# Layer 0's dense mixer of a two-layer trunk: both token streams in one pass over w1 and w3

## The chip, the cores and the metric

One NeuronCore of a Trainium2 chip runs the whole program. The metric is the device time of one execution in microseconds. A time is the median of several executions; the profile is of one more execution, and its span is counted from the first to the last instruction in it. Engines are named as in the profile: PE (products; PEld its weight loads), DVE and ACT (elementwise work), POOL, and SP, whose queue issues most DMAs.

## The reference, cut to what matters

Two streams of 256 tokens with 1024 features, the context and the latents, pass through a two-layer trunk. In a layer each stream is normed and modulated, goes through a token mixer (attention, a recurrence "RWKV", and a long convolution "Hyena"), a post-norm, a feature mixer and a second post-norm. Layer 0's feature mixer is dense and acts on both streams; layer 1's is a mixture of 8 experts and acts on the latents alone. Layer 1's context is needed only for the keys and values and for the recurrence's last state, from which the latents' recurrence starts.

```
o_lat, o_ctx = token_mixer(modulate(x, sh1, sc1), modulate(xc, csh1, csc1), ...)
x  = post_norm(alpha * x  + g1  * o_lat, ln1_g, ln1_b)
xc = post_norm(alpha * xc + cg1 * o_ctx, ln1_g, ln1_b)          # layer 0 only
f_lat = swiglu(modulate(x, sh2, sc2), w1, w3, w2)               # layer 0; layer 1: experts
f_ctx = swiglu(modulate(xc, csh2, csc2), w1, w3, w2)            # layer 0 only
x, xc = post_norm(alpha * x + g2 * f_lat, ...), post_norm(alpha * xc + cg2 * f_ctx, ...)

swiglu(h, w1, w3, w2) = (silu(h @ w1) * (h @ w3)) @ w2          # 1024 -> 2816 -> 1024
```

## The kernel before, in words

**Products.** All matrices are float32. Each operand is split into a rounded high part and a low rest (`split`: a cast on ACT, L315, and a subtraction on DVE, L316), and `mm3` issues three products for one (high x high, high x low, low x high; L321 to L323). In the profile a weight block is `wraw` as loaded and `whi`, `wlo` as split; `hp` is a stream's normed, modulated and transposed input, split.

**Loads.** `wload` fetches one block of 128 x 1024 (512 KB), splits it and returns the two parts. `raw` queues the loads on SP, each behind the one before (`behind`), so loads go out in the order of the program. In the stretch spoken of here the buffers are those of `BUFS["l"]`: 6 for raw blocks and 4 pairs for split ones; the latents of layer 1 use other ones, `"n"` (5 and 4). If `s.fill` is set, each `wload` also advances a generator by a step: `ada` of layer 1 (48 loads, each followed by four small products, tile `ada`).

**Order.** The order of the instructions on each engine is fixed when the program is built. A scheduler picks it: of the instructions that it holds to be ready it takes the one that the program wrote first, so later work fills what earlier work leaves open, as far as buffers allow. `s.order(a, b)` keeps `a` behind `b` in that order. PSUM has eight banks: three tagged `g`, two `a`, and `w0`, `w1`, `t`.

**Layer 0's feature mixer.** `ffn(l, st, x)` is a generator for one stream. `hT` (L443) norms the 256 tokens (`xhat`), transposes them on PE (tile `hT`), modulates on DVE (`hf`) and splits into `hp`. `block(b, hp)` (L1319) computes 256 of the 2816 hidden features: four loads of w1 and w3, 24 products with 256 columns (the tokens) each, into two `g` banks (tile `ab`); then silu and the gate, split into `ffg`. The products with w2 (tile `fo`, 512 columns) are made in two parts, of six and five blocks; a part has two halves of the output, `tok_mm` goes through its loads, 12 products each. `post_norm` (L1218) reads each half's banks on DVE, adds to the residual `pnr`, and norms at the end; `tok_last` orders the last half's products so that the first 128 tokens end earlier.

**The sequence in `body`.** The context's `w_out` of layer 0 and the latents' Hyena; the context's hT for the mixer (`some(f, 1)`); the latents' `w_out` with its post-norm; the whole mixer of the context, with `ada` as fill; ten steps of the latents' mixer (hT, six blocks, their w2 products, one more block); then layer 1 of the context: its input products `win` (tile `u`, seven tiles), `rw_prep`, and the recurrence `rwkv` for both directions without output, `spectra` (Hyena's filters, tiles `hf_d`, `hf`, `hyK`); then the rest of the latents' mixer, which thus fills the recurrence's gaps; then layer 1 of the latents: hT, `win`, `rw_prep`, `rwkv`, attention, Hyena, `w_out`, and the experts.

**The recurrence.** A direction `d` uses the bank `w0` or `w1`. `rw_dir` ends in a chain of eight small products and updates (`rS`); L1096 copies the context's final state. `fed` is the last instruction that prepares a chain's inputs (L1075). `spectra` uses `w0`, `t` and `w1`, and `rw_prep` uses `w0` (tile `rw`).

## Time and profile before

| | us |
|---|---|
| median of 3 runs | 2133.1 |
| the three runs | 2117.61 to 2138.04 |
| the profiled execution | 2134.47 |
| its span | 2132.7 |
| mean granted clock of PE | 0.965 of full |

The span and what lies around it (1.8 us) make the profiled execution's time. A clock of 1.00 is 2.4 GHz, 0.50 is 1.2 GHz; a mean between them is a mixture of the two in time. The stretch of the change runs from about 518 us (the last product of the latents' `w_out`) to about 1092 (the latents' input products of layer 1); the first product of the experts is at 1338.1. In a windows view the first column is the window, then its length, then busy us and instructions (x) of each engine that has any, the mean clock, the share and the rate of DMA. In a timeline a row is start, duration, engine, line, operation, out<-in; the durations of products overlap, so their pace is the distance of starts.

### The profile page before, as it was taken

The page shows a single profiled execution, that of the slowest core. Times are in us where ns is not written, and L with a number is a line of the kernel's source. Part 1 is how long each engine was busy: PE and PEld are TensorE (multiplying, and loading weights), DVE is VectorE, ACT ScalarE, POOL GpSimd, SP SyncE. Part 2 cuts the span into 40 slices and gives each one's busy share as a digit, 9 for nine tenths or more (in the row PEclk, how much of TensorE's full clock was granted, in tenths as well). Part 3 has the DMA queues.
Part 4 walks back from the last instruction along what each step waited for, and adds up shares of the span by engine and source line. Part 5 has one row for each costly group of instructions (what it writes and reads, how often), then busy time and mean ns, then how long its engine had stood idle before and what let it go on. Part 6 is the DMA issues. An engine that isn't in the chain of part 4 may idle for free. (4 is left out here: it accounts for less than half of the span.)

```text
span 2132.7 us, 35433 instructions
## 1 busy us (share of the span) xinstructions
PE 2033.8 (95%) x13514; PEld 1656.6 (78%) x13514; DVE 1659.7 (78%) x3050; ACT 1105.6 (52%) x1615; POOL 111.1 (5%) x87
## 2 busy tenths in 40 slices
PE   7999999999999999989798997999999999999996
PEld 2878777667878999888487676888888888888885
DVE  6897678469753685776888568799899989988997
ACT  3532445132332434443254232877787877778773
POOL 0012002100000000010101200000000000000000
PEclk9999899899999999999998997999999999999998
DMA  8522332246697545332311038699999999999992
GB/s 302 186 83 90 139 124 83 80 160 230 235 337 269 198 164 200 137 102 94 125 55 38 31 110 316 233 329 356 352 347 367 356 343 347 365 359 339 364 352 103
DMA packets 147850, 469.12 MB, mean 220 GB/s; under 512 B 31636, under 2 KB 33972, under 8 KB 147672
## 3 DMA queue, kind: packets, MB, share of 16 engines
q1 hardware_dynamic: 123512, 446.27, 57.9%
q0 software_dynamic: 4816, 17.36, 2.3%
q10 hardware_dynamic: 19344, 3.15, 0.8%
q8 instruction: 108, 1.77, 0.3%
q14 instruction: 70, 0.57, 0.1%
HBM read 464.56 MB, written 2.16 MB: 219 GB/s over the span
## 5 line engine op out<-in xcount | busy, mean ns | idle before, releaser
L316 DVE TENSOR_TENSOR wlo<-wraw,whi 128x1024 fp32r<-128x1024 f32 x748 | 887.4, 1221 | 83.0 <-ACT whi L315 52.4
L315 ACT CAST whi<-wraw 128x1024 fp32r<-128x1024 f32 x748 | 751.6, 1049 | 146.1 <-DMA wraw<-in_fw_dram 33.8
L321 PE MATMUL ab<-whi,m_x 128*128 128x512 f32 x704 | 281.6, 400 | 0.0
L323 PE MATMUL ab<-whi,m_x 128*128 128x512 f32 x704 | 275.6, 391 | 0.0
L322 PE MATMUL ab<-wlo,m_x 128*128 128x512 f32 x704 | 275.0, 391 | 0.0
L321 PE MATMUL ab<-hp,whi 128*128 128x256 f32 x704 | 204.9, 292 | 3.1 <-ACT hp L315 2.2
L323 PE MATMUL ab<-hp,wlo 128*128 128x256 f32 x704 | 201.8, 288 | 2.8 <-DVE wlo L316 2.8
L322 PE MATMUL ab<-hp,whi 128*128 128x256 f32 x704 | 201.4, 286 | 1.3 <-DVE hp L316 1.2
L321 PE MATMUL u<-hp,whi 128*128 128x256 f32 x512 | 152.0, 300 | 3.9 <-ACT hp L315 3.0
L323 PEld LDWEIGHTS ab<-whi,m_x 128*128 128x128 f32 x704 | 132.2, 188 | 28.3
L322 PEld LDWEIGHTS ab<-wlo,m_x 128*128 128x128 f32 x704 | 132.5, 188 | 25.5 <-DVE wlo L316 0.2
L321 PEld LDWEIGHTS ab<-whi,m_x 128*128 128x128 f32 x704 | 132.2, 188 | 25.1
L321 PEld LDWEIGHTS ab<-hp,whi 128*128 128x128 f32 x704 | 135.7, 193 | 19.0 <-issue 10.6
L323 PE MATMUL u<-hp,wlo 128*128 128x256 f32 x512 | 149.0, 294 | 1.4 <-DVE wlo L316 1.1
L322 PE MATMUL u<-hp,whi 128*128 128x256 f32 x512 | 149.5, 295 | 0.0
L323 PEld LDWEIGHTS ab<-hp,wlo 128*128 128x128 f32 x704 | 136.1, 194 | 6.3 <-DVE wlo L316 3.9
L322 PEld LDWEIGHTS ab<-hp,whi 128*128 128x128 f32 x704 | 136.4, 194 | 2.0 <-DVE hp L316 1.8
L321 PE MATMUL mo<-whi,ffg 128*128 128x512 f32 x352 | 137.8, 391 | 0.0
L323 PE MATMUL mo<-whi,ffg 128*128 128x512 f32 x352 | 137.1, 390 | 0.0
L322 PE MATMUL mo<-wlo,ffg 128*128 128x512 f32 x352 | 137.0, 389 | 0.0
L969 POOL TENSOR_TENSOR rBD<-rAT,cst 128x1024 f32<-128x1024 f32 x28 | 67.2, 2408 | 937.7 <-DVE rTm L959 506.9
L321 PEld LDWEIGHTS u<-hp,whi 128*128 128x128 f32 x512 | 99.6, 196 | 18.2 <-issue 9.6
(396 smaller groups left out, 3536.3 us busy)
## 6 DMA issues: line engine op xcount, KB each, us to landing
wraw<-in_mw_dram SPq DMA_DIRECT2D x495, 512.0 KB, 5.6
wraw<-in_fw_dram SPq DMA_DIRECT2D x132, 512.0 KB, 5.7
wraw<-in_adaw_dram SPq DMA_DIRECT2D x96, 512.0 KB, 4.4
wraw<-in_win_dram SPq DMA_DIRECT2D x64, 512.0 KB, 5.1
wraw<-in_mw_dram POOLq DMA_DIRECT2D x33, 512.0 KB, 6.7
wraw<-in_wout_dram SPq DMA_DIRECT2D x24, 512.0 KB, 4.2
lngb<-in_rows_dram SPq DMA_DIRECT2D x12, 512.0 KB, 7.3
x<-in_xs_dram SPq DMA_DIRECT2D x8, 512.0 KB, 5.6
```

Source lines behind the costliest of these rows:

```text
L315: i = (s.nc.scalar.copy if eng == "a" else s.nc.vector.tensor_copy)(hi, src)
L316: return i, s.nc.vector.tensor_sub(lo, src, hi.bitcast(F32))
L321: mm(out, a[0], b[0], start=start, stop=False, **kw)
L322: mm(out, a[0], b[1], start=False, stop=False, **kw)
L323: mm(out, a[1], b[0], start=False, stop=stop, **kw)
L969: i = nc.gpsimd.tensor_mul(x.rearrange("p u (j t) -> p u j t", j=4), bc(ATu[:, :, m, None, :], [128, 8, 4, 32]), bc(mask.rearrange("p (j t ...
```

## The change

w1 and w3 are laid out in 22 half blocks of 128 hidden features, two loads each, of four k-tiles by 128 + 128 columns. The streams' inputs `hp` lie side by side in eight tiles of 512 tokens, so that one product takes both streams. Only the first three half blocks (`ALONE`) run by stream: the context's at once, the latents' after the first part. The w2 products come in three parts, of 6, 8 and 8 half blocks; the context's follow their part, the latents' first part too, and the latents' other two are written behind layer 1's context. `ab` banks alternate between `g` and `a`. `ada` fills the joint pass. `spectra` is written behind the latents' hT of layer 1, and order edges hold three things of layer 1's latents behind `fed`: Hyena's scaling on ACT, attention's first scores, and the first steps of `rw_out`.

```diff
-    A["fw13"] = w13(g("ffn_w1"), g("ffn_w3"))[0]
+    u = w13(g("ffn_w1"), g("ffn_w3"))[0].reshape(11, 2, 2, 128, 2, 2, 2, 128)
+    A["fw13"] = np.ascontiguousarray(u.transpose(0, 6, 1, 3, 2, 4, 5, 7)).reshape(22, 2, 128, 4, 256)
...
-    def hT(s, l, st, prm, src, f32=None):
-        nc = s.nc
-        dst = s.pairs("hp", "hp", "hp", "hp")
+    def hT(s, l, st, prm, src, dst=None):
+        nc = s.nc
+        dst = dst or s.pairs("hp", "hp", "hp", "hp")
...
-    def conv3(s, u, out, cp, cc, cn, bias):
+    def conv3(s, u, out, cp, cc, cn, bias, after=None):
...
+        if after is not None:
+            s.order(i, after)
...
-        s.conv3(ps, o, s.pv(l, "hw0", i), s.pv(l, "hw1", i), s.pv(l, "hw2", i), s.pv(l, "hb", i))
+        s.conv3(ps, o, s.pv(l, "hw0", i), s.pv(l, "hw1", i), s.pv(l, "hw2", i), s.pv(l, "hb", i),
+                g.get("hyfed"))
...
-    def attend(s, l, g, oT):
+    def attend(s, l, g, oT, read=None):
...
-        half, read = [slice(0, 64), slice(64, 128)], None
+        half = [slice(0, 64), slice(64, 128)]
...
+        g["fed"] = fed
...
-        nc.vector.tensor_add(pr, kf[:, 0], kf[:, 1])
+        i = nc.vector.tensor_add(pr, kf[:, 0], kf[:, 1])
+        if l == 1:
+            s.order(i, g["fed"])
...
-        nc.scalar.activation(sg[64:96], lo[64:96, :], AF.Tanh, scale=0.5)
+        i = nc.scalar.activation(sg[64:96], lo[64:96, :], AF.Tanh, scale=0.5)
+        if l == 1:
+            s.order(i, fed)
...
-    def post_norm(s, l, st, which, x, parts, apart=()):
+    def post_norm(s, l, st, which, x, parts, apart=(), pause=False):
...
+                if pause:
+                    yield
...
-    def block(s, b, hp):
-        nc = s.nc
-        ps = [s.bank("g", "ab") for _ in range(2)]
-        for kh in range(4):
+    def block(s, b, hp, hs, gt, sts):
+        nc = s.nc
+        both = len(sts) == 2
+        ps = [s.bank("ga"[b % 2], "ab") for _ in range(2 if both else 1)]
+        src = hp if both else hs[sts[0]]
+        out = ps if both else [ps[0][:, :256], ps[0][:, 256:]]
+        for kh in range(2):
             hi, lo = s.wload(s.A["fw13"][b, kh])
-            for n, p in enumerate(ps):
-                for f in range(2):
-                    for k in range(2):
-                        ws = slice(512 * k + 256 * n + 128 * f, 512 * k + 256 * n + 128 * f + 128)
-                        s.mm3(p[:, 256 * f:256 * f + 256], (hi[:, ws], lo[:, ws]), hp[2 * kh + k],
-                              kh == 0 and k == 0 and f == 0, kh == 3 and k == 1, skip_group_check=True)
-        t = s.k([128, 512], "ffs")
-        nc.scalar.activation(t, ps[0], AF.Tanh, scale=0.5)
-        nc.vector.scalar_tensor_tensor(t, t, 1.0, ps[0], op0=OP.add, op1=OP.mult)
-        nc.vector.scalar_tensor_tensor(t, t, 0.5, ps[1], op0=OP.mult, op1=OP.mult)
-        g = s.k([128, 2, 2, 256], "ffg", F32R)
-        s.split(t.rearrange("p (f t) -> p f t", f=2), g[:, 0], g[:, 1])
-        return g[:, 0], g[:, 1]
+            for n, p in enumerate(out):
+                for k in range(4):
+                    ws = slice(256 * k + 128 * n, 256 * k + 128 * n + 128)
+                    s.mm3(p, (hi[:, ws], lo[:, ws]), src[4 * kh + k], kh == 0 and k == 0 and (both or n == 0),
+                          kh == 1 and k == 3, skip_group_check=not both)
+        w = 256 * len(sts)
+        t = s.k([128, 512], "ffs")[:, :w]
+        nc.scalar.activation(t, out[0], AF.Tanh, scale=0.5)
+        nc.vector.scalar_tensor_tensor(t, t, 1.0, out[0], op0=OP.add, op1=OP.mult)
+        nc.vector.scalar_tensor_tensor(t, t, 0.5, out[1], op0=OP.mult, op1=OP.mult)
+        for i, st in enumerate(sts):
+            g = s.k([128, 2, 256], f"ffg{st}", F32R)
+            s.split(t[:, 256 * i:256 * i + 256], g[:, 0], g[:, 1])
+            gt[st][b] = g[:, 0], g[:, 1]
...
-    def ffn(s, l, st, x):
-        hp = s.hT(l, st, 3, x)
-        yield
-        def part(b0, n):
-            gt = []
+    PARTS, ALONE = ((0, 6), (6, 8), (14, 8)), 3
+    def ffn_in(s):
+        t = [s.k([128, 2, 512], "hp", F32R) for _ in range(8)]
+        cut = lambda st: [(h[:, 0, 256 * st:256 * st + 256], h[:, 1, 256 * st:256 * st + 256]) for h in t]
+        return [(h[:, 0], h[:, 1]) for h in t], [cut(CTX), cut(LAT)]
+    def ffn(s, l, hp, hs, x):
+        gt = {}, {}
+        def part(st, n):
+            b0, nb = s.PARTS[n]
             def o(h):
-                for b in range(b0, b0 + n) if h == 0 else ():
-                    gt.append(s.block(b, hp))
-                    yield
-                t2 = lambda i, k: tuple(gt[k // 2][m][:, k % 2, 128 * i:128 * i + 128] for m in range(2))
-                banks = [s.bank("g", "fo") for _ in range(2)]
-                src = lambda kh: s.A["fw2"][h, b0 + kh]
-                if h == 1 and b0 > 0:
-                    s.tok_mm(src, t2, banks, 2 * n, range(n - 3))
-                    s.tok_last([(src(kh), kh, banks) for kh in range(n - 3, n)], t2, 2 * n)
+                t2 = lambda i, k: tuple(q[:, 128 * i:128 * i + 128] for q in gt[st][b0 + k])
+                banks = [s.bank("ga"[h] if n < 2 - st else "g", "fo") for _ in range(2)]
+                src = lambda kh: s.A["fw2"][h, b0 // 2 + kh]
+                nc = nb // 2
+                if h == 1 and n == 2:
+                    s.tok_mm(src, t2, banks, nb, range(nc - 3))
+                    s.tok_last([(src(kh), kh, banks) for kh in range(nc - 3, nc)], t2, nb)
                 else:
-                    s.tok_mm(src, t2, banks, 2 * n)
+                    s.tok_mm(src, t2, banks, nb)
                 yield
                 return banks
             return o
-        return (yield from s.post_norm(l, st, 1, x, [part(0, 6), part(6, 5)], (1,)))
+        out = [s.post_norm(l, st, 1, x[st], [part(st, n) for n in range(3)], (1,), True) for st in range(2)]
+        for b in range(s.ALONE):
+            s.block(b, hp, hs, gt, (CTX,))
+        s.hT(0, LAT, 3, x[LAT], hs[LAT])
+        for n, (b0, nb) in enumerate(s.PARTS):
+            for b in range(max(b0, s.ALONE), b0 + nb):
+                s.block(b, hp, hs, gt, (CTX, LAT))
+            if n == 0:
+                for b in range(s.ALONE):
+                    s.block(b, hp, hs, gt, (LAT,))
+            if n < 2:
+                s.some(out[CTX], 4)
+            if n == 0:
+                s.some(out[LAT], 4)
+        return s.whole(out[CTX]), out[LAT]
...
-        f = s.ffn(0, CTX, x[CTX])
-        s.some(f, 1)
+        hp, hs = s.ffn_in()
+        s.hT(0, CTX, 3, x[CTX], hs[CTX])
         x.append(s.w_out(0, 1, oT[1], None))
         s.fill = s.ada(1, [0, 1, 2])
-        xc = s.whole(f)
+        xc, f = s.ffn(0, hp, hs, x)
         s.drain()
-        f = s.ffn(0, LAT, x[LAT])
-        s.some(f, 10)
         s.ldlora(1)
         gc = {"st": CTX, "h": s.hT(1, CTX, 0, xc)}
         s.win(1, [0, 1, 2, 3, 4, 5, 6], gc)
         s.rw_prep(1, gc)
         S0 = s.rwkv(1, gc, None, None)
-        for _ in s.spectra(1, "w0", "t", "w1", *s.spec_load(1)()):
-            pass
+        sp = s.spec_load(1)
         x = s.whole(f)
         s.w = "n"
         gl = {"st": LAT, "h": s.hT(1, LAT, 0, x)}
+        for _ in s.spectra(1, "w0", "t", "w1", *sp()):
+            pass
         oT = s.pairs("oTa", "oTa", "oTr", "oTh")
         s.win(1, RW, gl)
         s.rw_prep(1, gl)
         s.rwkv(1, gl, S0, oT)
+        gl["hyfed"] = gl["fed"]
         s.win(1, ATT + HY[:2], gl)
-        s.go(s.attend(1, gl, oT))
+        s.go(s.attend(1, gl, oT, gl["fed"]))
         s.win(1, HY[2:], gl)
         s.go(s.hyena(1, gl, oT))
         x = s.w_out(1, LAT, oT, x)
```

## Rows read from the trace of the kernel before

**Rows 1.** The profile page, busy time of the engines (share of the span, instructions).

```profile
PE 2033.8 (95%) x13514; PEld 1656.6 (78%) x13514; DVE 1659.7 (78%) x3050; ACT 1105.6 (52%) x1615; POOL 111.1 (5%) x87
```

**Rows 2.** Windows, stages of the stretch: PE, PEld, DVE, ACT, POOL busy; PEclk; DMA.

```profile
518.00:746.00 228.00, 226.58 (x1718) 187.46 (x1713) 133.39 (x207) 79.94 (x94) 0.00 (x0) 1.00 0.72 259
746.00:868.00 122.00, 118.54 (x834) 111.76 (x833) 84.37 (x144) 49.33 (x61) 0.00 (x0) 0.97 0.50 184
868.00:1007.00 139.00, 130.91 (x1294) 117.48 (x1293) 100.81 (x239) 60.55 (x114) 13.31 (x8) 0.99 0.28 92
1007.00:1054.00 47.00, 45.66 (x166) 28.91 (x164) 39.12 (x55) 20.21 (x23) 6.73 (x2) 1.00 0.44 147
1054.00:1070.00 16.00, 2.20 (x9) 1.43 (x8) 14.68 (x58) 0.00 (x0) 0.00 (x0) 0.62 0.32 105
1070.00:1092.00 22.00, 21.51 (x164) 21.29 (x163) 18.47 (x35) 15.02 (x26) 0.00 (x0) 0.89 0.22 72
1092.00:1300.00 208.00, 194.39 (x1649) 155.75 (x1648) 143.58 (x394) 76.67 (x155) 23.65 (x14) 0.93 0.25 81
```

**Rows 3.** Timeline of PE, 256 columns: first and last of 85 in a row.

```profile
779.73 0.28 PE L322 MATMUL ab<-hp,whi 128*128 128x256 f32 x1
...
789.81 0.28 PE L322 MATMUL ab<-hp,whi 128*128 128x256 f32 x1
```

**Rows 4.** Timeline of PE, 512 columns: first and last of 31 in a row.

```profile
504.64 0.39 PE L322 MATMUL wo<-wlo,oTa 128*128 128x512 f32 x1
...
511.44 0.39 PE L322 MATMUL wo<-wlo,oTh 128*128 128x512 f32 x1
```

**Rows 5.** Windows of tile ab (products with w1, w3): PE, PEld, DVE, ACT busy.

```profile
518.00:746.00 228.00, 136.09 (x1056) 128.64 (x1056) 15.10 (x22) 6.58 (x11) 1.00 0.72 259
868.00:1007.00 139.00, 56.24 (x376) 48.60 (x375) 4.90 (x8) 2.39 (x4) 0.99 0.28 92
```

**Rows 6.** Windows of tile fo (products with w2): PE, PEld, DVE busy.

```profile
518.00:746.00 228.00, 63.57 (x264) 48.48 (x264) 4.75 (x7) 1.00 0.72 259
```

**Rows 7.** Lines, 518 to 746: the two casts of a weight block.

```profile
L316 DVE TENSOR_TENSOR wlo<-wraw,whi 128x1024 fp32r<-128x1024 f32 x65 | 77.3, 1217 | 8.7 <-ACT whi L315 8.7
L315 ACT CAST whi<-wraw 128x1024 fp32r<-128x1024 f32 x66 | 66.6, 1046 | 37.2 <-DMA wraw<-in_fw_dram 29.4 <-PE fo L323 4.6 <-PE fo L322 3.1
```

**Rows 8.** Waits of PE, 500 to 1100: us in total, times, longest.

```profile
PE ab L323 <- DVE wlo L316: 2.8, 4, 1.4
```

**Rows 9.** Timeline of DVE, 542 to 560: end of the latent norms.

```profile
543.72 1.26 DVE L1266 SCALAR_TENSOR_TENSOR x<-x,keep,lngb 128x1024 f32<-128x1024 f32 x1
...
556.45 0.81 DVE L441 TENSOR_SCALAR xhat<-x,keep 128x1024 f32<-128x1024 f32 x1
```

**Rows 10.** Windows, the two stalls before a transposed input.

```profile
746.00:758.00 12.00, 8.54 (x46) 7.47 (x45) 12.00 (x36) 2.57 (x5) 0.00 (x0) 0.72 0.00 0
1054.00:1075.00 21.00, 6.71 (x29) 5.73 (x29) 19.05 (x68) 2.43 (x6) 0.00 (x0) 0.59 0.24 80
```

**Rows 11.** Timeline of PE around the latent tail.

```profile
1053.80 0.39 PE L323 MATMUL fo<-whi,ffg 128*128 128x512 f32 x1
1066.60 0.69 PE L455 MATMUL hT<-keep,xhat 128*128 128x128 f32 x2 [12.41 <-DVE xhat L441]
...
1070.71 0.58 PE L321 MATMUL u<-hp,whi 128*128 128x256 f32 x1 [0.49 <-ACT hp L315]
```

**Rows 12.** Timeline of PE, first input product of the layer 1 context.

```profile
869.97 0.39 PE L321 MATMUL u<-hp,whi 128*128 128x256 f32 x1 [0.86 <-ACT hp L315]
```

**Rows 13.** Timeline of ACT, last copy of the context state.

```profile
1006.69 0.29 ACT L1096 COPY keep<-rS 128x128 f32<-128x128 f32 x1
```

**Rows 14.** Tile hf_d: the decays of the spectra, first and last start.

```profile
L548 PE MATMUL hf_d<-hydec,cst x8: 587/874/1216, 7.7 to 1006.9; 1*128 1x512 f32 x8
```

**Rows 15.** Tile hyK: the last piece of the spectra, first and last start.

```profile
L609 DVE SCALAR_TENSOR_TENSOR hyK<-hy_rb,cst,hyK x2: 730/732/735, 46.4 to 1041.7; 1x512 f32<-1x512 f32 x2
```

**Rows 16.** Timeline of PE, first product of the latent rw_prep.

```profile
1093.87 1.12 PE L855 MATMUL rw<-lora,rkl 33*128 33x512 f32 x2
```

More of the change, by code (lines that the diff above doesn't have):

```diff
@@ L483, in win_steps @@
             yield
-    def conv3(s, u, out, cp, cc, cn, bias):
+    def conv3(s, u, out, cp, cc, cn, bias, after=None):
         nc = s.nc
         if bias is None:
-            nc.scalar.activation(out, u, AF.Copy, scale=cc)
+            i = nc.scalar.activation(out, u, AF.Copy, scale=cc)
         else:
-            nc.scalar.activation(out, u, AF.Identity, scale=cc, bias=bias)
+            i = nc.scalar.activation(out, u, AF.Identity, scale=cc, bias=bias)
+        if after is not None:
+            s.order(i, after)
         nc.vector.scalar_tensor_tensor(out[:, 1:], u[:, :255], cp, out[:, 1:], op0=OP.mult, op1=OP.add)
@@ L1148, in rw_out @@
         nc = s.nc
-        vt, kf, kT = g["vt"], g["kf"], g["kT"]
+        vt, kf, kT, fed = g["vt"], g["kf"], g["kT"], g["fed"]
         pr = s.k([128, 2, 256], "rro")
-        nc.vector.tensor_add(pr, kf[:, 0], kf[:, 1])
+        i = nc.vector.tensor_add(pr, kf[:, 0], kf[:, 1])
+        if l == 1:
+            s.order(i, g["fed"])
         nc.vector.tensor_mul(pr, pr, kT)
```

## The prediction

> **What bounds the kernel now.** I read the page's busy times first: PE 95%, DVE 78%, ACT 52% [rows 1]. A total cannot say what one stage is worth, so next the windows of the stretch that the change touches, 518 to 1092 us, and of the one behind it [rows 2]. PE is nearly closed in the context's mixer (226.6 of 228 us), in the first part of the latents' (118.5 of 122) and in layer 1's context part (130.9 of 139). It is open in one place: 1054 to 1070, where 2.2 of 16 us are PE's and DVE works for 14.7. So most of the stretch costs what PE's stream costs, and the rest is that tail.
>
> What the stream costs is the distance between starts, not the duration of a row, since products overlap. With 256 columns 84 steps take 10.08 us, so 120.0 ns [rows 3]; with 512 columns 30 steps take 6.80 us, so 226.7 ns [rows 4].
>
> **The wider products.** A load of a w1/w3 half block is used by 24 products. Before there are 88 such loads, all with 256 columns, 1056 products per stream [rows 5]. After: 12 loads by one stream alone and 38 by both. 912 products of 512 columns replace 1824 of 256, and 912 x (2 x 120.0 - 226.7) ns = **12.1 us** less. The w2 products stay (264 of 512 columns per stream [rows 6]). The Trainium skill would have it otherwise: "TensorE: Matmul & The Clock Gate", section "Back-to-back issue gap", gives an isolated gap of N/2.4 + 2.5 ns, so that two narrow products cost only 2.5 ns more than a wide one. By that page the estimate is 912 x 2.5 ns = 2.3 us. The trace disagrees so far: 120.0 ns where the page has 109.2.
>
> **Fewer loads.** 38 loads of 512 KB go, and with each a cast of 1.05 us on ACT and a subtraction of 1.22 us on DVE [rows 7]: 40 and 46 us of engine time. I cost this at nothing: over 600 us PE waited 2.8 us for those low halves [rows 8], which is the bound. Without PE's cover it would be the whole 46 us, but a load is followed by 24 products (2.9 or 5.4 us) and prepared in 1.22.
>
> **The latents' transposed input, early.** Before, hT of the latents stands between the two mixers: 12.0 us with 8.5 busy at a mean clock of 0.72 [rows 10], so 6.7 us at 1.2 GHz, of which some 4.5 held products that took twice as long: 3.5 + 2.2 = 5.7 us lost. After, it must be ready when three half blocks of the context are done. These end at 518 + 144 x 0.120 + 2 for the context's hT + an eighth of the 41.5 us that ada's products and the rest take in 518 to 746 (228 - 1056 x 0.120 - 264 x 0.2267) = 542.5. DVE finishes the latents' x at 545.0 and, before the change, their xhat at 557.3, among casts for later blocks [rows 9]. The new xhat lies between; the casts ahead are bounded by four cast buffers, so I take 550 and the first product at 551. PE stands 8.5 us, plus the same 2.2 at half clock: 10.7, a net **+5** (bounds -1, if x alone decides, and +14, if xhat comes as before).
>
> **Two tails.** After, the context's last w2 product ends both mixers' main part. It is at 518 + 17.3 + 17.3 (alone) + 206.7 (912 wide) + 59.8 + 16.3 (w2 of the context, and of the latents' first part) + 41.5 + 10.7 + 2 = 890. What could fill PE then, the latents' last 16 w2 loads, is written behind the seven w_in loads of layer 1's context; loads go out in order, and those seven take all four pairs of cast buffers until hT of the context is there. So the context gets the tail that the latents have now: 1053.8 (last product) to 1070.7 (first input product), PE waiting 12.4 us for xhat [rows 11], the clock at 0.59 around it [rows 10]. The latents' own tail comes later, under the context's recurrence or just behind it. How much of it shows? Layer 1's context part takes 136.7 us from its first input product to the copy of its state, 870.0 to 1006.7 [rows 12, 13]. In it 376 narrow products (45.1 us by pace) filled PE [rows 5]; now 192 wide ones (43.5 us) do. So the fill ends near the end of the chain, not well before it, and I take 5 us of the tail as open (0 to 14). PE's idle time, 868 to 1092: before 8.1 + 1.3 + 13.8 + 0.5 = 23.7 us [rows 2]. After 14.3 (context tail, with the 0.5 behind it) + 8.1 + 5 = 27.4: **+3.7** (-9 if tail and chain both close by the moved spectra, +13 if the tail is all open).
>
> **The fill itself.** The 376 narrow products occupied 56.2 us in the chain against 45.1 by pace [rows 5]: 11 us went in short groups whose last product is not overlapped. Half as many instructions, twice as long, should lose less: **-4** (0 to -11).
>
> **Spectra and the new order edges.** The spectra of layer 1 move from the context part to behind the latents' hT. Their instructions stay: DMAs, PE, ACT and DVE alike; their first loads are still issued where they were, the last one after the latents' loads. Their long part begins when the second direction's bank is free, 1006.9, and ends at 1041.7 [rows 14, 15]. After, the state is copied at 890 + 16.9 + 136.7 = 1044, so they would end near 1079, or some 5 later because DVE shares them with the latents' hT. rw_prep of the latents needs their bank; it began at 1093.9 [rows 16], and would begin near 1084. That second way of counting gives -10 at this point, beside -7.4 by PE's ledger up to here (-12.1 + 5 + 3.7 - 4). The order edges keep attention and Hyena of the latents (ACT's scaling, the first scores, rw_out's first steps) behind the last `fed`. Behind these on ACT and DVE wait only w_out's inputs, needed at the end. PE is idle for 13.6 us in 1092 to 1300 at a clock of 0.93 [rows 2]; a chain with fewer strangers on DVE may win a part, and fill that comes too late may lose one: **-4** (-13.6 to +10).
>
> **Sum.** -12.1 + 5 + 3.7 - 4 - 4 = -11.4 us against the profiled execution's 2134.5 (span 2132.7): 2123. The median of the three runs is 1.4 lower, so 2122. A measurement of this kernel tells about 1%, 21 us, from no change; its own three runs differ by that much.
>
> **Rivals.** (A) Everything overlaps: x decides the early hT and no stall is left (-10.7), the latents' tail is wholly covered (-5), and most of the idle time behind 1092 closes (another -9.6): -36.7, so 2096. For it: from the context's chain on, the latents' norm, hT, input products and spectra are all free to fill. Against it: the fill of 43.5 us is no larger than what the chain swallowed before. (B) Slower: the spectra become a bar before the latents' rw_prep. They come before it in priority, need both recurrence banks, and so start at 1044; if DVE serves the latents' tail (14.7 us) and the stretch of input products (18.5 us) [rows 2] between their steps instead of beside them, they end at 1044 + 34.8 + 33.2 = 1112, 18 us after 1093.9, and what follows shifts by that: 2151. It decides from where the context's state is later than 1026 with DVE full. For it: DVE is busy 14.7 of 16 and 18.5 of 22 us there. Against it: half of the spectra is PE and ACT work. (C) The wide products don't pay: a wide product costs nearly two narrow ones in a mixed stream, and some 10 us of the 12.1 don't come: 2132. Against it: rows 3 and 4, both from this kernel. That is the time that the page's rule would give, too.
>
> **How the numbers follow.** Forecast 0.45 (its own range 2110 to 2138), A 0.33, B 0.14, C 0.05, other 0.03. Faster by over 1% (below 2111.8): A and a little of the forecast, 0.37. Slower by over 1% (above 2154.4): the far half of B and most of the rest, 0.10. Within 1%: 0.53. The range goes from below A, 2088, to B's time, 2151.
>
> **What would show it.** Right: w1/w3 products of 512 columns in steps of 0.227 us, 912 of them, and 288 of 256; 94 loads of the mixer instead of 132; PE idle for 4 to 17 us near 543 and for about 14 with a falling clock near 890, with the last w2 products of the latents inside the context's chain; rw_prep of the latents near 1084. Wrong: a context tail filled by other products (then A); the step of wide products near 0.24 (C); spectra running past 1095 while PE idles (B); a new wait on `ffg` or `hp` buffers inside the mixer, which I cost at nothing since I found no row for it.

## The result, and the profile after

The changed kernel takes 2160.0 us (median of 4 runs, 2155.5 to 2164.8) where the kernel before takes 2135.6 beside it: a ratio of 1.0132, 95% interval 1.0095 to 1.0169, so some 24 us slower. The profiled execution took 2157.7 us, its span is 2155.9.

The page's busy times, which answer to [rows 1]: every engine works less than before, TensorE by 4 us, and the program is longer.

```profile
PE 2029.5 (94%) x12602; PEld 1609.8 (75%) x12602; DVE 1630.5 (76%) x3056; ACT 1072.0 (50%) x1600; POOL 107.8 (5%) x87
```

The windows of the stages, cut where the stages now begin; they answer to [rows 2].

```profile
509.00:543.00 34.00, 27.33 (x230) 20.86 (x230) 33.80 (x94) 9.70 (x17) 0.00 (x0) 0.96 0.79 272
543.00:877.00 334.00, 334.00 (x1716) 258.92 (x1714) 154.57 (x218) 101.06 (x143) 0.00 (x0) 0.99 0.49 175
877.00:897.00 20.00, 2.67 (x11) 1.46 (x9) 18.67 (x65) 0.43 (x2) 0.00 (x0) 0.61 0.18 60
897.00:1035.00 138.00, 125.46 (x1085) 105.06 (x1085) 97.53 (x228) 54.96 (x100) 13.38 (x8) 0.96 0.29 95
1035.00:1066.00 31.00, 16.24 (x43) 7.84 (x43) 28.97 (x95) 7.99 (x14) 0.39 (x1) 0.61 0.05 17
1066.00:1100.00 34.00, 34.00 (x198) 26.16 (x198) 29.21 (x44) 16.11 (x25) 2.72 (x2) 0.96 0.25 93
1100.00:1327.00 227.00, 206.69 (x1650) 164.15 (x1648) 147.54 (x399) 76.88 (x155) 23.88 (x14) 0.89 0.23 83
```

Read it from the open places. The joint pass, 543 to 877, is closed to the last microsecond. In front of it 6.7 us are open. Behind it stand two tails, 877 to 897 and 1035 to 1066, with VectorE busy and TensorE at a mean clock of 0.61. The last window, layer 1's latents, has as many products as in the kernel before (1650 for 1649 in its window of [rows 2]) and takes 17 us longer.

To compare kernels I use two stages, read from the timelines. The **mixer stage** goes from the first w1/w3 product (before 518.2, after 508.8) to the latents' rw_prep (1093.9 and 1099.6): 575.7 before, 590.8 after. **Layer 1's latents** go from there to the router's first product (1303.8 and 1327.0): 210.0 and 227.4. What follows takes 829 us in both. 15.1 + 17.4 us, less 9.4 for the earlier start, are the 23.2 by which the spans differ; the start is no part of the change (last section).

TensorE's idle time in the mixer stage (the stage, less each product's distance to the next start or, if shorter, its own duration) goes from 28.6 us to 51.3, its work from 547.1 to 539.5. So the change does less work, as meant, and leaves three times that saving open. Where, TensorE's waits from 500 to 1330 say (total, times, longest):

```profile
PE hT L457 <- DVE xhat L443: 21.8, 4, 15.3
PE hf L579 <- ACT sn L517: 8.1, 1, 8.1
PE hf L561 <- ACT sn L517: 6.2, 1, 6.2
PE rPQ L1036 <- DVE rTT L1025: 5.6, 2, 5.1
```

The context's tail and the latents' tail on TensorE's timeline; they answer to [rows 11] and [rows 12].

```profile
877.02 0.39 PE L325 MATMUL fo<-whi,ffg 128*128 128x512 f32 x1
892.73 0.69 PE L457 MATMUL hT<-keep,xhat 128*128 128x128 f32 x2 [15.32 <-DVE xhat L443]
895.00 1.54 PE L457 MATMUL hT<-keep,xhat 128*128 128x128 f32 x6 [1.58 <-DVE xhat L443]
896.97 0.58 PE L323 MATMUL u<-hp,whi 128*128 128x256 f32 x1 [0.43 <-ACT hp L317]
...
1037.15 0.40 PE L325 MATMUL fo<-whi,ffg 128*128 128x512 f32 x1
...
1047.10 1.11 PE L561 MATMUL hf<-sn 64*64 64x256 f32 x2 [6.21 <-ACT sn L517]
1056.30 2.07 PE L579 MATMUL hf<-hy,sn 64*128 64x512 f32 x2 [8.09 <-ACT sn L517]
1058.30 0.47 PE L457 MATMUL hT<-keep,xhat 128*128 128x128 f32 x1
...
1065.39 0.56 PE L323 MATMUL u<-hp,whi 128*128 128x256 f32 x1
```

Between the last w2 product of the context and its transposes TensorE gets nothing at all. The latents' last w2 product comes at 1037, just after the context's chain has ended (last copy of its state at 1035.7), so their tail too has nothing beside it but the spectra, two steps of which wait 6.2 and 8.1 us for ScalarE's sines.

### The profile page after: what moved, and what is told of

Its sections match the earlier page's. It is cut to its first block, busy times and chain, and to the rows that moved or that the text cites. A ratio compares the mean times of both kernels' runs of the same rounds, so it can differ in the third digit from the quotient of the medians.

```text
span 2155.9 us, 33468 instructions
## 1 busy us (share of the span) xinstructions
PE 2029.5 (94%) x12602; PEld 1609.8 (75%) x12602; DVE 1630.5 (76%) x3056; ACT 1072.0 (50%) x1600; POOL 107.8 (5%) x87
## 5 line engine op out<-in xcount | busy, mean ns | idle before, releaser
L318 DVE TENSOR_TENSOR wlo<-wraw,whi 128x1024 fp32r<-128x1024 f32 x710 | 843.4, 1221 | 76.7 <-ACT whi L317 52.6
L317 ACT CAST whi<-wraw 128x1024 fp32r<-128x1024 f32 x710 | 716.1, 1049 | 131.5 <-DMA wraw<-in_fw_dram 22.8
L323 PE MATMUL ab<-hp,whi 128*128 128x512 f32 (+1 forms) x400 | 148.6, 372 | 0.0
L325 PE MATMUL ab<-hp,wlo 128*128 128x512 f32 (+1 forms) x400 | 145.6, 364 | 2.2 <-DVE wlo L318 2.2
L324 PE MATMUL ab<-hp,whi 128*128 128x512 f32 (+1 forms) x400 | 145.8, 365 | 0.0
L323 PEld LDWEIGHTS u<-hp,whi 128*128 128x128 f32 x512 | 101.0, 198 | 21.3 <-issue 10.9
L324 PEld LDWEIGHTS u<-hp,whi 128*128 128x128 f32 x512 | 101.0, 198 | 2.1 <-issue 1.3
L325 PEld LDWEIGHTS u<-hp,wlo 128*128 128x128 f32 x512 | 100.7, 198 | 2.0 <-issue 1.5
L1350 DVE SCALAR_TENSOR_TENSOR ffs<-ffs,ab 128x512 f32<-128x512 f32 (+1 forms) x25 | 15.5, 622 | 106.7 <-ACT ffs L1349 106.7
```

The costliest lines, as they stand in the source:

```text
L317: i = (s.nc.scalar.copy if eng == "a" else s.nc.vector.tensor_copy)(hi, src)
L318: return i, s.nc.vector.tensor_sub(lo, src, hi.bitcast(F32))
L323: mm(out, a[0], b[0], start=start, stop=False, **kw)
L324: mm(out, a[0], b[1], start=False, stop=False, **kw)
L325: mm(out, a[1], b[0], start=False, stop=stop, **kw)
L1350: nc.vector.scalar_tensor_tensor(t, t, 1.0, out[0], op0=OP.add, op1=OP.mult)
```

## The experiments

One table first; the sections then refer to it. Stages and idle time come from each kernel's one profiled execution, medians and ratios from the runs. A ratio is taken beside the kernel before on the same chip, whose medians there were 2128.9 to 2131.5 for the x, e, y and z kernels; so a median of one row is not to be set against that of another. e3's four runs lie between 2111.7 and 2147.9, too far apart for a ratio; it is read from its profile alone.

| kernel | mixer stage (idle) | layer 1's latents | median (runs) | ratio, 95% interval |
|---|---|---|---|---|
| before | 575.7 (28.6) | 210.0 | 2135.6 (4) | |
| after | 590.8 (51.3) | 227.4 | 2160.0 (4) | 1.0132, 1.0095 to 1.0169 |
| x1 no edges | 591.3 (50.9) | 208.4 | 2147.2 (10) | 1.0083, 1.0046 to 1.012 |
| x2 edges alone | 575.9 (28.5) | 229.0 | 2153.2 (10) | 1.0094, 1.0057 to 1.013 |
| x3 spectra back | 588.0 (47.4) | 226.1 | 2159.5 (4) | 1.0127, 1.005 to 1.0203 |
| x4 mixer alone | 587.0 (46.1) | 205.9 | 2141.4 (10) | 1.0056, 1.0014 to 1.0098 |
| e1 attend's edge | 575.7 (28.7) | 217.7 | 2139.5 (10) | 1.0063, 1.0036 to 1.009 |
| e2 convolution's edge | 576.0 (28.8) | 218.3 | 2135.2 (10) | 1.0029, 0.9995 to 1.0063 |
| e3 gates' edges | 576.0 (28.3) | 218.7 | | |
| y1 more fill | 584.6 (44.9) | 211.4 | 2138.7 (9) | 1.0035, 1.0012 to 1.0059 |
| y4 own buffers | 588.2 (42.6) | 209.5 | 2146.1 (4) | 1.0094, 1.0075 to 1.0113 |
| y5 six alone | 584.5 (45.2) | 205.7 | 2134.0 (10) | 1.0023, 0.9994 to 1.0051 |
| y10 = y4 + y5 | 586.0 (40.6) | 206.2 | 2144.1 (4) | 1.0095, 1.0066 to 1.0125 |
| z1 = y1 + y5 | 580.7 (38.0) | 206.3 | 2133.3 (10) | 1.0019, 0.9989 to 1.0049 |
| z2 = z1, spectra back | 584.0 (46.4) | 212.4 | 2135.0 (10) | 1.0016, 0.9988 to 1.0045 |
| z3 three beside tail | 573.6 (32.2) | 212.5 | 2127.8 (10) | 0.998, 0.9945 to 1.0015 |
| z4 six beside tail | 562.5 (22.6) | 209.9 | 2115.8 (8) | 0.9903, 0.9862 to 0.9945 |
| z5 = z3, spectra back | 573.3 (38.8) | 206.0 | 2124.9 (10) | 0.9951, 0.9924 to 0.9979 |
| z7 = z4, spectra back | 563.7 (27.7) | 205.6 | 2114.5 (5) | 0.9919, 0.9888 to 0.9951 |
| z8 eight beside tail | 564.2 (25.3) | 208.9 | 2122.0 (8) | 0.9953, 0.9915 to 0.999 |

The x, y and z kernels are the changed one with the edits named, except x2; all y and z kernels are without order edges. x2 and the e kernels are the kernel before with edges.

How firm is one execution? The five kernels with the mixer of the kernel before agree on the mixer stage within 0.3 us, after and x1 within 0.5. Layer 1's latents are looser: without edges they take 205.6 to 212.5 us in fourteen kernels, so a difference of a few us in that column says nothing.

**The parts of the change (x1 to x4).** x1 takes the three order edges out of the changed kernel, x2 puts them into the kernel before, x3 puts the spectra back, x4 does both and so leaves the joint mixer alone.

```diff
 # x1
-                g.get("hyfed"))
+                None)
-        if l == 1:
-            s.order(i, g["fed"])
 ...
-        s.go(s.attend(1, gl, oT, gl["fed"]))
+        s.go(s.attend(1, gl, oT))
 # x3
-        sp = s.spec_load(1)
+        for _ in s.spectra(1, "w0", "t", "w1", *s.spec_load(1)()):
+            pass
         x = s.whole(f)
 ...
```

x1: 

> The changed kernel with the three order edges of layer 1's latents taken out; the mixer and the moved spectra stay. Stage lengths are read from the trace: mixer (first w1/w3 product to the latents' rw_prep, 576 us before, 591 after) and latents' layer 1 (rw_prep to the experts' first small product m_lc, 210 before, 227 after). Theory: the edges take attention and Hyena out of the recurrence's gaps and put them behind it, so the second stage falls to 210 to 215, the time by about 15 us, to 2145. Rival: the second stage is longer because the moved spectra and the later start leave DVE full; then it stays at 225 to 229 and the time at 2160.

x2: 

> The kernel before with the three order edges and nothing else. Theory: the latents' layer 1 grows from 210 to 222 to 227 us and the time by 12 to 17, to about 2150. Rival (the edges are harmless without the moved spectra): 208 to 213 us, no change that can be measured.

x3: 

> The changed kernel with the spectra where they were, ahead of the latents' remaining w2 products; the edges stay. Theory: beside the latents' norm on DVE the spectra stretch the tail between the last w2 product and the first input product (28 us after, 17 before); it falls to 17 to 19, the mixer stage from 591 to about 580, the time to about 2150. Rival: the tail is long because the norm is, and the spectra only cost elsewhere what they cost here: the mixer stage stays within 3 us of 591.

x4: 

> The changed kernel with the edges out and the spectra back: the joint mixer alone. Theory: its own ledger (12 us from the wide products, against two open tails and the stall of the early transposed input) is near zero: mixer stage 573 to 582, latents' layer 1 208 to 213, time 2128 to 2142. Rival: the joint mixer itself is the loss (a context tail that nothing can fill), then the mixer stage stays at 587 to 593 and the time at 2145 or above.

Measured: with the edges layer 1's latents take 226.1 to 229.0 us, without them 205.9 to 210.0, on either kernel. Pair by pair (x2 and before, after and x1, x3 and x4) the edges cost 19 to 20 us of that stage and touch no other. Where the spectra stand is worth 3 to 4 us of the mixer stage. The joint mixer alone makes that stage 11 to 12 us longer, edges or not. x1 and x2 went as their theories had it, within 2 us of the stage; x3 and x4 went in the stage as their rivals had it, since the tails stay open wherever the spectra stand. So there are two causes, and they add: the kernel after carries both.

**How an edge costs (e1, e2, e3).** Each is the kernel before with one of the edges.

```diff
 # e1: attend's first scores       s.go(s.attend(1, gl, oT, gl["fed"]))
 # e2: conv3's first pass on ACT   + if after is not None: s.order(i, after)
 # e3: rw_out's sum and tanh       + if l == 1: s.order(i, g["fed"])
```

e1: 

> The kernel before with the order edge of attend alone (the keys' products and what follows them wait for the state's last N; the convolution and the gates without edge). Theory (what costs is that attention, which stood ready as fill from 1153 on, is kept until 1204, so that TensorE has nothing beside the state's steps): layer 1's part of the latents (from the last rw_prep to the router's first product) goes from 210 to 225 to 229 us, the run by 15 to 19 us above the kernel before, as with all edges. Rival (the gates' tanh, which is first on ScalarE's queue and waits 18.8 us there, costs it): 208 to 213 us, the run within 4 us of the kernel before.

e2: 

> The kernel before with the order edge of the latents' convolution alone (ScalarE's first pass of each of its channels waits for the state's last N). Theory (the three edges add up: all cost 19.0 us, attention's 7.7, the gates' 8.7): 211 to 214 us for the latents' part of layer 1, the run 0 to 5 us above the kernel before. Rival (each edge by itself already keeps most of the fill away, and they only overlap): 217 to 220 us, the run 6 to 10 us above.

e3: 

> The kernel before with the two order edges in rw_out alone (the sum of the keys' halves on VectorE and the gates' tanh on ScalarE wait for the state's last N). Theory (attention's edge costs, see the run before this): 208 to 213 us for the latents' part of layer 1, the run within 4 us of the kernel before. Rival (the tanh blocks ScalarE's queue, with casts and evictions behind it): 222 to 229 us, the run 13 to 19 us above the kernel before.

Measured: 217.7, 218.3 and 218.7 us, so each alone costs some 8 us of the stage, neither all of it nor nothing. Theory and rival missed in e1 and in e3; in e2 the rival had the stage right. The sum of the three (24.8) is more than all together (19.0), so they seem to overlap, though the scatter of that stage leaves this open. In e1 the run's time shows the cost (1.0063); in e2 it doesn't (1.0029, with 1 inside the interval), and only the profile tells. One thing that an edge can do shows in ScalarE's waits, of the kernel after and of e2, which have the same wait at another instruction:

```profile
ACT rof L1190 <- PE rN L1076: 18.8, 1, 18.8
```

```profile
ACT hvx L491 <- PE rN L1074: 18.6, 1, 18.6
```

The instruction that has the edge stands on ScalarE's queue before others and holds them: behind `rof` come two of the convolution's `hvx`. In the kernel before, the gates' `rof` ran at 1085.1; in the kernel after it runs at 1204.3, and attention's first scores come at 1204.6 instead of 1152.7. But that wait is not what all edges have in common. e1 and e3 don't have it: in e1 the edge is on a product, and attention's first scores are merely put later (100 us behind rw_prep instead of 59); in e3 `rof` runs at 1182.6 without a wait. They cost as much. What is common to all is the clock while the state's last steps run. The same 34 us (from 107 us behind rw_prep on) in e3 and in the kernel before:

```profile
1188.00:1222.00 34.00, 34.00 (x156) 21.92 (x155) 14.19 (x36) 8.46 (x19) 2.34 (x1) 0.50 0.10 32
```

```profile
1201.00:1235.00 34.00, 33.88 (x319) 22.82 (x318) 16.91 (x41) 8.29 (x21) 2.15 (x1) 0.90 0.13 47
```

In e3 TensorE is idle for less of the stage than in the kernel before (12.0 us for 13.6), and the stage is 8.7 us longer all the same. Over those 34 us the mean clock is 0.50 to 0.80 in the six kernels with edges (e1 0.70, e2 0.80); without edges it is 0.90 to 1.00 in twelve, and 0.80 in z2 and z3, whose stage is the longest of the fourteen. Windows of the same stretch in the kernel after and in x1:

```profile
1205.00:1215.00 10.00, 9.34 (x93) 7.12 (x89) 7.93 (x14) 1.13 (x3) 2.43 (x1) 0.70 0.00 0
1215.00:1225.00 10.00, 9.21 (x48) 6.51 (x41) 3.19 (x12) 3.72 (x9) 0.00 (x0) 0.50 0.01 2
1225.00:1240.00 15.00, 15.00 (x45) 7.93 (x46) 5.97 (x18) 3.00 (x9) 0.00 (x0) 0.50 0.00 0
```

```profile
1205.00:1215.00 10.00, 10.00 (x140) 8.52 (x137) 6.33 (x10) 1.75 (x5) 4.68 (x2) 1.00 0.17 53
1215.00:1225.00 10.00, 9.88 (x60) 5.89 (x58) 6.90 (x20) 4.15 (x11) 0.00 (x0) 1.00 0.30 107
1225.00:1240.00 15.00, 15.00 (x165) 11.07 (x165) 6.11 (x17) 3.58 (x9) 0.00 (x0) 0.98 0.01 1
```

TensorE is busy in both, but in the kernel after at 1.2 GHz, with 45 products in the last 15 us instead of 165. Over the whole stage the length times the mean granted clock is nearly the same, 227.4 x 0.89 = 202 us and 208.4 x 0.96 = 200: all but a few of the 19 us between these two kernels is clock. "Busy" alone would not have shown it. That edges and a lower clock go together is what these rows show; which of the work put off brings the clock down, and why the gates alone do it in e3, where attention comes early, they don't.

**Fill, buffers and the early wait (y1, y4, y5, y10).** y1 leaves the latents' first w2 part for layer 1's chain too; y4 gives layer 1's context the other set of load and cast buffers; y5 runs six half blocks by stream before the joint ones; y10 is y4 and y5.

```diff
 # y1
-            if n == 0:
-                s.some(out[LAT], 4)
 # y4
+        s.w = "n"
         s.win(1, [0, 1, 2, 3, 4, 5, 6], gc)
+        s.w = "l"
 # y5
-    PARTS, ALONE = ((0, 6), (6, 8), (14, 8)), 3
+    PARTS, ALONE = ((0, 6), (6, 8), (14, 8)), 6
```

y1: 

> The changed kernel without its order edges, and the latents' first six half blocks' w2 products are moved behind layer 1's context too (before: at once behind the context's first part). The work of TensorE stays the same; the fill beside the context's chain grows by 48 wide products of some 0.26 us, about 12 us, and the context's tail comes that much earlier. Theory (the two tails are paid open, because nothing is queued beside them; the fill in the context's chain only has to end before that chain does): the chain had 13 us of idle time in 897 to 1035 which more fill can cover, so the mixer stage (first gate product to the latents' rw_prep) falls from 591 by 5 to 12 us, and the run from 2147 to 2135 to 2142. Rival (fill of any amount is spread over the chain and ends with it, so the latents' tail stays as open as it was and the chain is lengthened by what is added): mixer stage 588 to 594, run 2144 to 2150.

y4: 

> The changed kernel without its order edges, and layer 1's context takes the other set of cast buffers for its own weights, so that the latents' w2 products and the context's weights don't share one. Theory (nothing stands ready beside the context's tail, 17 of whose 20 us at 877 are idle, since the latents' products are only issued inside the chain): the buffers are not what holds them; mixer stage 588 to 592, run 2145 to 2149. Rival (the shared buffers hold the fill back, and with it w2 products reach the tail and the idle spots of the chain): idle time of the mixer stage 51 falls to 35 to 40, stage 575 to 580, run 2131 to 2136.

y5: 

> The changed kernel without its order edges, with six half blocks instead of three run for the context alone. Theory (the wait of the wide products for the latents' normalization costs 6 to 7 us of idle time in 508 to 543, less 1.9 us for the three more half blocks in narrow products): that idle time goes to 1 to 2, mixer stage 586 to 588, run 2142 to 2145. Rival (the wait is only moved, since w_out of the latents and its normalization run beside the blocks at whatever place DVE comes to them): idle in the first 60 us unchanged within 2, stage 591 to 594, run 2147 to 2151.

y10: 

> The two edits before this one together (own cast buffers for layer 1's context, six half blocks alone; no order edges). Theory: the sum of the two, mixer stage 584 to 589, run 2140 to 2146, which is not below the kernel before (2131 to 2136). Rival (buffers and early wait both hold the kernel back): stage 571 to 576, run 2127 to 2132, level with the kernel before or ahead of it.

Measured: y1 went as the theory had it, 6.7 us off the stage (with a fill of 72 products more, not 48); the chain's idle time fell from 12.7 us in x1 to 8.0 and the latents' tail's from 14.8 to 12.3. y4 went as the theory had it too, in the stage (588.2) and in the run: the window of its context's tail is as open as before,

```profile
887.00:907.00 20.00, 2.23 (x8) 1.43 (x8) 18.79 (x66) 1.10 (x2) 0.00 (x0) 0.59 0.37 134
```

so the buffers are not what keeps fill from the tail. By 892.2 four blocks of the latents' w2 are cast there, which in the kernel after wait until layer 1's input products run; still TensorE's next product is the transpose at 903.4, and the first w2 product comes at 932.9: in TensorE's order it stands behind layer 1's first input products. Why the order was built so stays open. y4's idle time did fall, by 8.3 us (50.9 to 42.6), in the chain and in the latents' tail, but its products took 5.2 us longer, so 3.1 came out. y5 took the early idle time from 6.2 us to 2.2, and the stage by 6.8, a little more than the theory; y10 went as its theory had it and shows that the buffers add nothing to y5.

**Both together, and the spectra (z1, z2).**

z1: 

> The changed kernel without order edges, with the latents' first part of w2 products behind layer 1's context too and six half blocks alone: the two edits that took some 7 us each out of the mixer stage, together. Theory (they cover different idle time, the early wait in 508 to 543 and idle spots in the context's chain): mixer stage 575 to 579 (591.3 less 6.7 less 6.8), run 2124 to 2132, level with the kernel before. Rival (both cover the same idle time, since either has 45 us of it): mixer stage 583 to 586, run 2133 to 2139.

z2: 

> As the run before this, and the spectra back at their old place ahead of the latents' tail. Theory (the spectra's six transforms in the latents' tail wait 14 us for ScalarE's sines; at the old place these waits lie in the context's chain, which has more to do now, and the tail has VectorE to itself): mixer stage 570 to 575, run 2120 to 2128, ahead of the kernel before by 2 to 10 us. Rival (the place of the spectra is worth the 3 us seen without fill, and gives them back as the tail then has nothing on TensorE): mixer stage 575 to 581, run 2125 to 2133.

Measured: z1's 580.7 falls between its two expectations; z2's 584.0 is worse than both. The gains overlap in part, the spectra's old place does not help, and the tail of 20 us with 17 of them idle is still there in every one of these kernels.

**Products beside the context's tail (z3, z4, z5, z7, z8).** The latents' half blocks by stream, which ran inside the pass, are written behind the context's last w2 products; there are three of them (z3), six (z4) or eight (z8).

```diff
 # z4
+    PARTS, ALONE = ((0, 6), (6, 8), (14, 8)), 6
-            if n == 0:
-                for b in range(s.ALONE):
-                    s.block(b, hp, hs, gt, (LAT,))
-            if n == 0:
-                s.some(out[LAT], 4)
-        return s.whole(out[CTX]), out[LAT]
+        xc = s.whole(out[CTX])
+        for b in range(s.ALONE):
+            s.block(b, hp, hs, gt, (LAT,))
+        return xc, out[LAT]
```

z3: 

> The changed kernel without order edges; the latents' three half blocks by stream are put behind the context's last w2 products, so that they stand ready while the context's second normalization runs, and the latents' first part of w2 follows the context's layer 1 as in the run with more fill. Theory (what the joint mixer loses is the context's tail: 17 of its 20 us idle where the kernel before had the latents' products beside it): three narrow half blocks are 3 x 48 products of 120 ns, 17 us; idle time of the tail falls to 2 to 5, mixer stage from 585 to 569 to 573, run 2122 to 2129, ahead of the kernel before. Rival (the tail is VectorE's, 18.7 of its 20 us busy, and the half blocks' gating and splitting on VectorE make it longer by what they take, 3 x 3 us and more; the tail ends later and the blocks' products are only moved): mixer stage 578 to 585, run 2132 to 2139.

z4: 

> As the run before this with six half blocks by stream. Theory: the early wait goes too (5 us idle, less 1.9 us of narrow products); 35 us of the latents' products stand behind the context's last, 17 beside its tail and 18 ahead of layer 1's first product, which only moves work; mixer stage 565 to 570, run 2118 to 2126. Rival (layer 1's context starts 18 us later, and its chain of 140 us sets the end, since the fill behind it is done before it): mixer stage 574 to 581, run 2128 to 2135.

z5: 

> As the first run of this call, with the spectra at their old place ahead of the latents' tail. Theory (with more fill the old place leaves the latents' tail 14 us idle, as in the run with six half blocks and the spectra back, where it cost 3 us): mixer stage 571 to 577, run 2124 to 2133. Rival (the latents' tail is shorter by the 8 us that the spectra take in it, and nothing is lost elsewhere): mixer stage 563 to 569, run 2116 to 2124.

z7: 

> As z4 (no order edges, six half blocks by stream, the latents' six beside the context's tail), with the spectra at their old place ahead of the latents' tail. Theory (the place of the spectra is worth 0 to 3 us either way, as it was with three half blocks: the eight us that the latents' tail loses are idle there instead): mixer stage 561 to 566 (z4: 562.5), run 2113 to 2120, within 0.3 % of z4. Rival (with 35 us of products behind the tail the context's chain has room for the spectra, and the latents' tail becomes shorter): mixer stage 552 to 558, run 2104 to 2111.

z8: 

> As z4 with eight half blocks by stream instead of six. Theory (the tail of some 20 us is covered with six already; the two more cost 1.3 us in narrow products and only push layer 1's context back by 12 us): mixer stage 562 to 567, run 2115 to 2121. Rival (what helps is the later start of layer 1's context, whose chain then stands beside less open work): mixer stage 550 to 557, run 2103 to 2111.

Measured: in the stage z3 came out at the edge of its theory, z4 2.5 us below its own, and z5, z7 and z8 within theirs. Against y1, which has the same work, z3 takes 11 us off the stage; z4 takes another 11 and is ahead of the kernel before by 1% (0.9862 to 0.9945). The windows of the tail, from the context's last w2 product to its first input product of layer 1, in z3 and then in z4:

```profile
851.00:880.00 29.00, 20.14 (x155) 19.15 (x154) 27.81 (x79) 9.20 (x15) 0.00 (x0) 0.85 0.54 181
```

```profile
832.00:868.00 36.00, 35.35 (x294) 35.08 (x292) 34.77 (x90) 16.32 (x25) 0.00 (x0) 1.00 0.63 220
```

The rival was right in one thing: with products beside it the tail gets longer, 29 us instead of 20, since the casts of the blocks' weights and their gates run on VectorE between its steps (nine weight casts in it, 10.9 us, for three in y1). But they don't only move: in z3 8.9 us of the 29 are open, against 17.4 of y1's 20; in z4 35.4 us of products fill 36. Six instead of three also end the early wait (2.3 us idle). Eight (z8) bring nothing more: the tail is already full. With the tail filled, the spectra's place is worth a microsecond of the mixer stage either way (z5 and z7 beside z3 and z4).

z4 and z7 are ahead of both kernels, at 2115.8 and 2114.5 us; z5 and z8 too, by half a per cent.

## Why the prediction was wrong

Forecast 2122.0, range 2088 to 2151, slower at 0.10; it came out at 2160. By its own steps, with the mixer stage's difference of +15.1 us (of which I had -7.4) and the next stage's +17.4 (of which I had -4, with the spectra) as the ledger:

- **The wider products: right.** TensorE's timeline in the joint pass, first and last of 55 in a row, for [rows 4]:

```profile
799.73 0.39 PE L323 MATMUL ab<-hp,whi 128*128 128x512 f32 x1
...
811.97 0.39 PE L323 MATMUL ab<-hp,whi 128*128 128x512 f32 x1
```

  12.24 us for 54 steps is 226.7 ns, so the 12.1 us were there. The Trainium skill's rule for an isolated product ("TensorE: Matmul & The Clock Gate", section "Back-to-back issue gap") would have made them 2.3, by estimate; neither trace agrees with it.
- **Fewer loads: right** at nothing. In 500 to 870 `ab` waits for a low half once, 2.2 us (before 2.8 [rows 8]).
- **The early hT: right in kind, a little dear.** Idle time at the start went from 1.4 us [rows 2] to 6.7, where I had 8.5, and the stall of 3.5 between the mixers is gone: +1.8 of idle time, and 1.0 more for hT's products at half clock, where I had a net +5. My upper bound, +14, comes to 11 or 12 by its own terms.
- **The fill: right in sum, by luck.** w1/w3 and w2 products together exceed their pace by 23.0 us before (270.2 + 125.9 less 2112 x 0.120 and 528 x 0.2267) and by 18.3 after (248.4 + 130.9 less 912 x 0.2267, 288 x 0.120 and 528 x 0.2267): -4.6, I had -4. But I had it inside the chain, and there nothing was gained; the window of tile fo there has 183 products at 291 ns, 11.8 us over their pace for 11 before, and the gain lies outside:

```profile
897.00:1035.00 138.00, 53.29 (x183) 33.45 (x183) 4.74 (x7) 0.96 0.29 95
```

- **Two tails: wrong.** I had 27.4 us of idle time from the context's tail on; it is 44.6. Of the 17.2 more, 3.0 are the context's tail (17.3 for 14.3), 4.4 the chain (12.5 for 8.1), and 9.8 the latents' tail, which I took as open for 5 us and which is open for 14.8. The step that failed is "so the fill ends near the end of the chain, not well before it, and I take 5 us of the tail as open": by that very reason the tail had to be open altogether, because a tail is covered only by work that is left when it begins. Against the kernel before this step is +20.9 where I had +3.7, beyond even my bound of +13. The reason for the context's tail was wrong as well: not the cast buffers keep fill out of it (y4), but that in TensorE's order no product stands there; z3 and z4 show that it can be filled. In the kernel before, the context's w2 products end at 746 and its normalization then has the latents' first blocks beside it: 8.5 of 12 us filled [rows 10], 118.5 of 122 in the whole window [rows 2]. Joining the streams takes that work away, since all gate products of both are done when the tail begins. So one open tail became two, which I had seen, and I counted on the second to close, which nothing did.
- **Spectra and order edges: wrong**, and the largest miss: -4 forecast. Products beside the open places run at half clock and cost +8.5 us more (`hf` 5.2 to 8.7, `hT` 7.9 to 10.8, `u` 42.4 to 44.5 us), which I had priced at the early hT alone: 4.2 of it in the latents' tail and just behind (the spectra's `hf`, and `u`), 3.2 in and behind the context's tail, 1.0 at the early hT. By the runs the spectra's new place costs 3 to 4 us (x3, x4). The edges cost 19 to 20 (the stage is 17.4 longer). The step that failed is "behind these on ACT and DVE wait only w_out's inputs, needed at the end". Behind them on ScalarE stood the convolution's first passes, and attention, convolution and gates were themselves the work that stood beside the state's steps; with it put off, the clock there is 0.50 to 0.80 for 0.90 in the kernel before. I had +10 as the worst and did not price the clock.

Sum of the mixer stage: -12.1 + 22.7 of idle time - 4.6 + 8.5 = +14.5, measured 15.1.

Rival A (all overlaps) failed at the same place as the forecast. Rival B gave a time near the measured one by another way: the spectra end at 1091.2, before the latents' rw_prep at 1099.6, TensorE is closed from 1066 on, and taking them back (x3, x4) returns 3 to 4 us; they are no bar. Rival C is excluded by the steps of 226.7 ns.

## What to carry to other kernels

When two streams are joined to save products, look first at what the one stream's products covered in the other's normalization: the products saved 12 us here and the newly opened tail alone left 17 idle, until a few blocks were kept apart and placed beside it (six of 22, without the edges: 1% ahead of the kernel before). An edge that only orders instructions is not free: ask what is queued behind it, and what TensorE has to do meanwhile. Price a stretch that loses its fill in clock too, not in idle time alone.

## What was not expected

The clock takes more than the idle time does: layer 1's latents are 19 us longer in x2 than in the kernel before, but length times mean granted clock is 229.0 x 0.88 = 201.5 against 209.9 x 0.93 = 195.2, so only 6 of the 19 are left when the clock is taken out; TensorE's idle time in the stage grows by 5.5 (13.6 to 19.1).

The start scatters by 16 us, as much as the change moved the mixer stage. In the kernel before and in e1, e2, e3 and x2, which share all of layer 0 with it, the first w1/w3 product comes between 505.2 and 521.2 us. The granted clock of the same stretches, in the kernel before and in e3, whose start was the earliest:

```profile
200.00:300.00 100.00, 99.33 (x763) 75.38 (x763) 67.04 (x187) 43.11 (x98) 0.69 (x1) 0.90 0.35 123
400.00:500.00 100.00, 96.93 (x624) 71.14 (x624) 61.26 (x151) 26.66 (x49) 2.67 (x2) 0.91 0.46 156
```

```profile
200.00:300.00 100.00, 99.33 (x839) 75.47 (x839) 72.56 (x194) 46.57 (x103) 2.02 (x1) 0.98 0.40 144
400.00:500.00 100.00, 97.76 (x651) 74.29 (x652) 70.67 (x177) 29.64 (x51) 1.90 (x1) 1.00 0.54 184
```

At equal busy time the one has a clock of 0.90 and 0.91 and the other 0.98 and 1.00. Why the clock falls in one execution and not in the other no run here shows; it is why stages are compared here, and runs only by their intervals.
